# Seven block products in place of eight in a feed-forward layer on one core

## The chip, the core and the metric

The kernel runs on one core of a Trainium2 chip. TensorE (PE) multiplies; its weight loads are PEld. VectorE (DVE), ScalarE (ACT) and GpSimd (POOL) work element by element, and SyncE's queue (SPq) issues the transfers. Each engine runs its own list of instructions in order and waits on semaphores for the others. The metric is device time in microseconds (us). All matmuls of this text multiply 128 x 128 weights with a stream of 256 to 576 columns.

## The reference

One layer of a decoder with two groups of tokens, 512 of a prompt and 64 of samples (8 sequences of 8). After two mixers come the two lines that matter here, with `D_MODEL = 1024` and `D_FF = 4096`, and the last norm:

```
f = relu(rmsnorm(h, ln2_g) @ w_ff1)     # h: 576 x 1024, w_ff1: 1024 x 4096
y = h + (f * f) @ w_ff2                 # w_ff2: 4096 x 1024
y = rmsnorm(y, ln_f_g)
```

## The kernel before

Everything is float32, held as two rounded parts: hi is the value as PE's 32-bit format (F32R) rounds it, and lo the rest. `split` (L105 to L107) makes them, ACT the hi by a copy (L106), DVE the lo by a subtraction (L107). A product takes three matmuls, hi by hi, hi by lo and lo by hi; all of them are issued by `mm` (L95). A weight piece of 128 x 512 is loaded (`raw`) and split into a unit `wu` of 2 x 512 columns.

The 576 tokens stand as columns of Hh and Hl (hi and lo of the normed h, 128 x 8 x 576). The feed-forward runs in 8 chunks of 512 hidden columns, 4 blocks `m` of 128. In a chunk, **up** (the first product) makes for each block and for each half of the tokens (288 columns) one PSUM sum over 8 blocks `k`: 4 x 2 x 8 x 3 = 192 matmuls of 288 columns. `square` (L1053 to L1062) turns the sums into relu squared, split into Fh and Fl; POOL stacks hi and lo of the 64 sample tokens side by side in Fst. **down** (the second product) makes, for each half `nh` of the 1024 output columns, sums of 512 columns for four token tiles of 128 (12 matmuls each) and for the sample tile, tile 4 (8 matmuls): 112 matmuls of 512 columns. `acc` adds a sum to the residual R[t] on DVE (L968); for tile 4 it takes an ACT copy (L971, `atmp`), a DVE add (L973, `atm2`) and a POOL add (L974).

The last chunk takes the tiles one by one, tile 4 first, both halves, and after each tile `last_norm`: ACT squares R[t] into `y` with a running sum (L1036), DVE and POOL make the reciprocal root (L143, L145), DVE scales into y (L1038) and SPq stores it. `y` has two buffers; the last tile uses buffers of its own, `yh`, and works in halves.

What sets the order: the framework simulates the program when it is built and writes each engine's list from that; the waits follow from the buffers. A pool gives a tag so many buffers, and a new tile in a buffer waits for the last user of the old one, a store included. The pools of this part: 8 buffers for units of the first weight, 8 for units of the second, 7 for `raw`, 2 for each tag of `evp` (atmp, atm2).

Of the kernel before, what the change touches and what calls it, by code (L numbers as in the profile page):

```python
# [90 lines left out]
def _body(ctx, tc, nc, I, O):  # L91
# [851 lines left out]
    pools['wraw'] = tpool("wraw2", 7)  # L943
    evp = tpool("evp", 2)
# [70 lines left out]
    def last_norm(t, final):
        rows = tsz[t]
        if final:

            y = [rp.tile([128, 512], F32, name="yh", tag=f"yh{h}", bufs=1) for h in range(2)]
            q = rp.tile([128, 512], F32, name="yq", tag="yq", bufs=1)  # L1020
            s2 = rp.tile([128, 2], F32, name="ss2", tag="ss2", bufs=1)
            ss = rp.tile([128, 1], F32, name="ssf", tag="ssf")
            for h in range(2):
                x = R[t][:, h * 512:h * 512 + 512]
                act.activation(q[:rows], x, AF.Square, accum_out=s2[:rows, h:h + 1])
                (dve if h else pool).tensor_tensor(y[h][:rows], x, gf[:rows, h * 512:h * 512 + 512], op=ALU.mult)
            dve.tensor_tensor(ss[:rows], s2[:rows, 0:1], s2[:rows, 1:2], op=ALU.add)
# [138 lines left out]
```

## Time and profile before

| | us |
|---|---|
| median of 3 runs | 828.01 (827.09 to 829.6) |
| profiled execution | 827.65 |
| its span | 825.9 |
| PE busy | 789.6 (96% of the span) |
| DVE busy | 442.7 (54%) |
| ACT busy | 353.4 (43%) |
| POOL busy | 176.7 (21%) |
| mean granted clock of PE | 0.987 |

The span is one execution from its first instruction to its last; 1.75 us lie around it in the profiled execution's time. Busy time of PE counts pipelined matmuls to their modelled ends, so that a busy PE may still be slowed by its operands. The feed-forward's 8 chunks lie from about 397 us to 818 us; the last norms follow.

### The profile page before, as it was taken

Reading aid. Unit: us, or ns where it says so; the run is one execution under the profiler, and the core shown is the slowest. Engines: PE = TensorE matmul, PEld = TensorE weight load, DVE = VectorE, ACT = ScalarE, POOL = GpSimd, SP = SyncE. Lnnn points to the kernel's source line nnn. Section 1 sums busy time; section 2 is a strip of 40 time slices with the busy share of each in tenths; the row PEclk is TensorE's granted clock in tenths of the full one; section 3 lists DMA queues with packets and bytes.
Section 4 is the critical chain, followed back from the end, with each engine's and each line's share of the span. In section 5 each row is a group of like instructions: output and inputs, shape, how many; then the busy total and the mean of one; then the engine's idle time right before and its main releaser. Section 6 shows DMA issues by size and latency. Waiting matters only on the chain.

```text
span 825.9 us, 13167 instructions
## 1 busy us (share of the span) xinstructions
PE 789.6 (96%) x4825; PEld 685.8 (83%) x4825; DVE 442.7 (54%) x980; ACT 353.4 (43%) x864; POOL 176.7 (21%) x219
## 2 busy tenths in 40 slices
PE   6989999999997998999989999999999999999996
PEld 5879888878675776778888998989989899898985
DVE  5345878888962347443756345163452634435325
ACT  6535478787842243432634232232322324232213
POOL 1103744454310116010211111111111111111112
PEclk9999999999997999999999999999999999999999
DMA  9771422000967545533324132041320413303003
GB/s 317 201 207 30 135 54 52 2 2 27 327 234 264 194 118 195 194 120 115 121 85 150 54 102 75 29 153 52 102 88 16 154 52 102 102 15 100 2 1 115
DMA packets 55187, 92.05 MB, mean 111 GB/s; under 512 B 7858, under 2 KB 19090, under 8 KB 54994
## 3 DMA queue, kind: packets, MB, share of 16 engines
q1 hardware_dynamic: 54866, 91.14, 34.8%
q8 instruction: 38, 0.62, 0.3%
q14 instruction: 27, 0.22, 0.1%
q0 software_dynamic: 256, 0.07, 0.0%
HBM read 86.92 MB, written 8.39 MB: 115 GB/s over the span
## 4 chain that ended last, share of the span: by engine, by line
PE 83%; DVE 7%; DMA 3%; ACT 3%; issue 2%; POOL 1%; POOLq 0%; SPq 0%; DVEq 0%; ACTq 0%
PE acc L95 52%; PE pcs L95 6%; PE pd L95 5%; PE o L95 4%; PE pu L95 3%; PE pq L95 3%; PE s L95 2%; PE tp L692 2%; DMA raw<-in_w_in 2%; DVE wu L107 1%; PE pc L95 1%; POOL wu L107 1%; DVE Q L522 1%; POOL rstd L145 1%; DMA raw<-in_w_ff 1%
## 5 line engine op out<-in xcount | busy, mean ns | idle before, releaser
L95 PE MATMUL acc<-Hh,wu 128*128 128x288 f32 x1024 | 204.9, 295 | 0.2 <-ACT Hh L106 0.2
L106 ACT ACTIVATE wu<-raw 128x512 fp32r<-128x512 f32 (+1 forms) x184 | 105.5, 614 | 152.6 <-PE acc L95 119.5
L95 PEld LDWEIGHTS acc<-Hh,wu 128*128 128x128 f32 x1024 | 164.3, 188 | 0.7 <-ACT Hh L106 0.4
L95 PE MATMUL acc<-wu,Fh 128*128 128x512 f32 x512 | 155.5, 389 | 0.0
L95 PE MATMUL acc<-Hl,wu 128*128 128x288 f32 x512 | 150.7, 295 | 0.0
L107 DVE TENSOR_TENSOR wu<-raw,wu 128x512 fp32r<-128x512 f32 x160 | 105.2, 695 | 47.2 <-ACT wu L106 47.2
L95 PEld LDWEIGHTS acc<-wu,Fh 128*128 128x128 f32 x512 | 95.7, 188 | 19.5
L95 PE MATMUL acc<-wu,Fl 128*128 128x512 f32 x256 | 97.1, 389 | 0.0
L95 PEld LDWEIGHTS acc<-Hl,wu 128*128 128x128 f32 x512 | 96.0, 188 | 0.3
L1059 DVE TENSOR_TENSOR f<-relu 128x576 f32<-128x576 f32 x32 | 24.2, 756 | 117.9 <-ACT relu L1058 117.9
L968 DVE TENSOR_TENSOR OTp<-acc,OTp 128x512 f32<-128x512 f32 x72 | 47.7, 687 | 62.4 <-PE acc L95 62.4
L1058 ACT ACTIVATE relu<-acc 128x288 f32<-128x288 f32 x64 | 26.2, 409 | 116.9 <-PE acc L95 116.9
L974 POOL TENSOR_TENSOR R<-atm,R 64x512 f32<-64x512 f32 x18 | 30.5, 1700 | 155.1 <-DVE atm L973 155.1
L95 PE MATMUL pd<-wu,AH 128*128 128x512 f32 (+1 forms) x192 | 55.2, 371 | 8.7 <-ACT wu L106 8.2
L95 PE MATMUL pcs<-G,w 128*128 128x256 f32 x256 | 61.5, 396 | 0.0
L1061 POOL CAST Fst<-Fh 128x64 fp32r<-128x64 f32 x32 | 23.5, 734 | 175.2 <-ACT Fh L106 118.7
L95 PEld LDWEIGHTS pcs<-G,w 128*128 128x128 f32 x256 | 49.7, 199 | 10.5 <-issue 3.6
L95 PEld LDWEIGHTS acc<-wu,Fl 128*128 128x128 f32 x256 | 48.1, 188 | 10.0
L95 PEld LDWEIGHTS pd<-wu,AH 128*128 128x128 f32 x192 | 34.7, 193 | 14.8 <-ACT wu L106 8.6
L668 ACT ACTIVATE P<-s,nm 128x32 f32<-128x32 f32 (+4 forms) x88 | 40.5, 464 | 14.5 <-DVE nm L667 14.0
L95 PE MATMUL acc<-wu,Hh 128*128 128x512 f32 x128 | 40.6, 397 | 0.0
L107 POOL TENSOR_TENSOR wu<-raw,wu 128x512 fp32r<-128x512 f32 (+1 forms) x24 | 30.8, 1301 | 44.2 <-ACT wu L106 44.2
(329 smaller groups left out, 1349.5 us busy)
## 6 DMA issues: line engine op xcount, KB each, us to landing
raw<-in_w_ff SPq DMA_DIRECT2D x128, 256.0 KB
G<-in_cache_kv SPq DMA_DIRECT2D x64, 256.0 KB
raw<-in_w_in SPq DMA_DIRECT2D x32, 256.0 KB
raw<-in_w_out SPq DMA_DIRECT2D x16, 256.0 KB
out_wins<-in_state_win_kv SPq DMA_DIRECT2D x8, 504.0 KB
xt<-in_x_t SPq DMA_DIRECT2D x8, 288.0 KB
x<-in_x_prompt SPq DMA_DIRECT2D x4, 512.0 KB
KW<-in_win_kt SPq DMA_DIRECT2D x4, 512.0 KB
```

Source lines behind the costliest of these rows:

```text
L95: pe.matmul(out, lhsT, rhs, start=start, stop=stop, skip_group_check=not first_in_bank)
L106: act.activation(hi, src, AF.Copy)
L107: eng.tensor_tensor(lo, src, hi.bitcast(F32), op=ALU.subtract)
L145: pool.tensor_tensor(r[:rows], ms[:rows], mhalf[:rows], op=ALU.pow)
L522: dve.tensor_tensor(Q[b, h, c0:c1], src, Q[a, h, c0:c1].bitcast(F32), op=ALU.subtract)
L668: act.activation(p_[:, c0:c0 + w], src, AF.Exp, bias=nm[:, br, g:g + 1], accum_out=l[:, br, g:g + 1])
L692: pe.transpose(t_[:w, g * 128:(g + 1) * 128], P[g][:, c0:c0 + w], ident)
L968: dve.tensor_tensor(R[t][:, c0:c0 + 512], p, R[t][:, c0:c0 + 512], op=ALU.add)
L974: pool.tensor_tensor(R[4][:, c0:c0 + 512], tm2, R[4][:, c0:c0 + 512], op=ALU.add)
L1058: act.activation(r[:, i * 288:i * 288 + 288], p[:, :288], AF.Relu)
L1059: dve.tensor_tensor(f2, r, r, op=ALU.mult)
L1061: pool.tensor_copy(Fst[:, m, 0:64], Fh[:, m, 512:576].bitcast(F32))
```

## The change

From the second chunk on, up is done by Strassen's scheme in Winograd's form: two blocks `m` of the hidden columns, two halves of `k` and the two halves of the tokens make 2 x 2 blocks, and seven products of 4 `k` blocks take the place of eight. The token sums T1, T2, T4 and T3 (which overwrites the second half of the tokens' upper `k`) are made once, on DVE and ACT, after the up of chunk 0: for each of 4 `k`, 14 DVE operations of 288 columns and 4 ACT copies. The weight sums are made for each pair of blocks: two loads of 512 KB (`fraw`), four DVE sums of 512 columns, and seven splits. The seven results are put together on DVE in `seven`. Chunk 0 stays as it was, but with its squares by halves.

To make room, buffers shrink: 6 `raw`, one buffer for each tag of `evp`, 6 units of the second weight in a ring (a chunk still uses 8), 8 units of the first weight in a ring (a pair uses 7), one `fraw` pair, and one buffer `y` for all five last norms, the final one too. The weight sum `s3` and the final norm's scratch `yq` take the tag `atmp`. The order of two sums of the out projection before the feed-forward is changed. The last tile's second half is done in two quarters of 256 columns.

```diff
-    pools['wraw'] = tpool("wraw2", 7)
-    evp = tpool("evp", 2)
+    pools['wraw'] = tpool("wraw2", 6)
+    evp = tpool("evp", 1)
-    fw2a = tpool("fw2a", 6)
-    fw2 = [fw2a] * 6 + [fw2b] * 2
+    fw2a = tpool("fw2a", 4)
+    fw2 = [fw2a] * 4 + [fw2b] * 2
+    ring, ring2 = itertools.cycle(fw), itertools.cycle(fw2)
...
-        for t, nh in ((0, 0), (1, 0), (2, 0), (3, 0), (0, 1), (1, 1), (2, 1), (3, 1), (4, 0), (4, 1)):
+        for t, nh in ((0, 0), (1, 0), (2, 0), (3, 0), (4, 0), (0, 1), (1, 1), (2, 1), (3, 1), (4, 1)):
...
+    def token_sums(k):
...
+        t1 = sub2((0, 1), (0, 0))
+        split(T[0][0][:, k], T[0][1][:, k], t1)
+        t2 = sub1((1, 1), t1)
+        split(T[1][0][:, k], T[1][1][:, k], t2)
+        t4 = sub1((1, 0), t2)
+        split(T[2][0][:, k], T[2][1][:, k], t4)
+        t3 = sub2((1, 1), (0, 1))
+        split(Hh[:, k, N2:NT], Hl[:, k, N2:NT], t3)
+    def weight_sums(m0):
+        raw = []
+        for i in range(2):
+            r = rp.tile([128, 4, 256], F32, name="fraw", tag=f"fraw{i}", bufs=1)
+            sp.dma_start(r, w_ff1[i * 512:i * 512 + 512, m0 * 128:m0 * 128 + 256].rearrange("(k p) m -> p k m", p=128))
+            raw.append(r)
+        us = [next(ring).tile([128, 2, 512], F32R, name="wu", tag="w") for i in range(7)]
...
+        s3 = evp.tile([128, 512], F32, name="s3", tag="atmp").rearrange("p (k m) -> p k m", k=4)
+        put(0, a11)
+        dve.tensor_tensor(s3, a11, a21, op=ALU.subtract)
+        dve.tensor_tensor(a21, a21, a22, op=ALU.add)
+        dve.tensor_tensor(a11, a21, a11, op=ALU.subtract)
+        put(1, a11)
+        put(2, s3)
+        put(3, a21)
+        put(4, a12)
+        dve.tensor_tensor(a12, a12, a11, op=ALU.subtract)
+        put(5, a22)
+        put(6, a12)
...
-            y = [rp.tile([128, 512], F32, name="yh", tag=f"yh{h}", bufs=1) for h in range(2)]
-            q = rp.tile([128, 512], F32, name="yq", tag="yq", bufs=1)
+            y = rp.tile([128, D], F32, name="y", tag="y", bufs=1)
+            y = [y[:, h * 512:h * 512 + 512] for h in range(2)]
+            q = evp.tile([128, 512], F32, name="yq", tag="atmp")
...
-        y = rp.tile([128, D], F32, name="y", tag="y")
+        y = rp.tile([128, D], F32, name="y", tag="y", bufs=1)
...
+        def seven(m):
+            us = weight_sums(c * KC + m)
...
+            def prod(p, i, x, more=False):
+                for k in range(4):
+                    wh, wl = (us[i][:, s, k * 128:k * 128 + 128] for s in range(2))
+                    for j, (w, y) in enumerate(((wh, x[0]), (wh, x[1]), (wl, x[0]))):
+                        mm(p, w, y[:, k], not more and k == 0 and j == 0, k == 3 and j == 2, not more)
...
+            prod(a, 0, half(H, 0, 0))
+            p1 = fs("p1")
+            act.activation(p1, a, AF.Copy)
+            prod(b, 1, T[1])
+            u = fs("u2")
+            dve.tensor_tensor(u, b, p1, op=ALU.add)
+            prod(cc, 2, half(H, 0, 1))
+            v = fs("v")
+            dve.tensor_tensor(v, cc, u, op=ALU.add)
+            prod(d, 3, T[0])
+            dve.tensor_tensor(v, d, v, op=ALU.add)
+            out(v, 1, 1)
+            prod(a, 4, half(H, 1, 0), True)
...
+            prod(cc, 5, T[2], True)
...
+            prod(d, 6, half(H, 1, 1), True)
...
+        if c == 0:
+            for k in range(4):
+                token_sums(k)
...
             for t in (4, 0, 1, 2, 3):
-                for nh in range(2):
-                    down(t, nh, vs[nh])
+                down(t, 0, vs[0])
+                for c0, n in (((0, 256), (256, 256)) if t == 3 else ((0, 512),)):
+                    down(t, 1, vs[1], c0, n)
                 last_norm(t, t == 3)
```

The products are called P1 to P7 here, P1 being `prod(a, 0, ...)` and P7 `prod(d, 6, ...)`.

**Between two chunks, DVE.** Before, DVE's list goes from the last sums of a down through units of the coming weights (wu_6084 to wu_6099) and the sample tile's add (L973) to the first square of the next chunk:

```order
L107 TENSOR_TENSOR wu_6084<-raw_6082,wu_6084 128x512
L107 TENSOR_TENSOR wu_6089<-raw_6087,wu_6089 128x512
L107 TENSOR_TENSOR wu_6094<-raw_6092,wu_6094 128x512
L973 TENSOR_TENSOR atm2_5710<-acc_5699,atmp_5708 64x512
L107 TENSOR_TENSOR wu_6099<-raw_6097,wu_6099 128x512
L1059 TENSOR_TENSOR f2_5857<-relu_5856 128x576
L107 TENSOR_TENSOR Fl_5754<-f2_5857,Fh_5753 128x576
```

Of the change, at the start of chunk 3, wu_6652 to wu_6737 are units of the second weight; s3_6351, the two lines on fraw_6340 (L1066, L1067) and wu_6345 (the unit of P2) follow the sample tile's add:

```order
L107 TENSOR_TENSOR wu_6652<-raw_6650,wu_6652 128x512
L107 TENSOR_TENSOR wu_6657<-raw_6655,wu_6657 128x512
L107 TENSOR_TENSOR wu_6732<-raw_6730,wu_6732 128x512
L973 TENSOR_TENSOR atm2_6334<-acc_6323,atmp_6332 64x512
L107 TENSOR_TENSOR wu_6737<-raw_6735,wu_6737 128x512
L1065 TENSOR_TENSOR s3_6351<-fraw_6340 128x512
L1066 TENSOR_TENSOR fraw_6340<-fraw_6340,fraw_6342 128x4x128
L1067 TENSOR_TENSOR fraw_6340<-fraw_6340 128x4x128
L1072 TENSOR_TENSOR fraw_6342<-fraw_6342,fraw_6340 128x4x128
L107 TENSOR_TENSOR wu_6345<-fraw_6340,wu_6345 128x512
L107 TENSOR_TENSOR wu_6346<-s3_6351,wu_6346 128x512
L107 TENSOR_TENSOR wu_6347<-fraw_6340,wu_6347 128x512
```

The weight sums now stand behind the add of the sample tile, whose `atmp` holds the buffer that `s3` takes, and all units but those of P1 and P5 stand behind them.

**In the last down, PE.** Before, each token tile's two sums follow each other, and each is finished before the next begins (acc_8438 and acc_8452 are one tile, acc_8475 the next):

```order
L95 MATMUL acc_8438<-wu_8304,Fh_8048 128x512 x2
L95 MATMUL acc_8438<-wu_8304,Fl_8049 128x512
L95 MATMUL acc_8452<-wu_8309,Fh_8048 128x512 x2
L95 MATMUL acc_8452<-wu_8309,Fl_8049 128x512
L95 MATMUL acc_8452<-wu_8314,Fh_8048 128x512 x2
L95 MATMUL acc_8452<-wu_8314,Fl_8049 128x512
L95 MATMUL acc_8452<-wu_8319,Fh_8048 128x512 x2
L95 MATMUL acc_8452<-wu_8319,Fl_8049 128x512
L95 MATMUL acc_8452<-wu_8324,Fh_8048 128x512 x2
L95 MATMUL acc_8452<-wu_8324,Fl_8049 128x512
L95 MATMUL acc_8475<-wu_8289,Fh_8048 128x512 x2
```

Of the change, wu_8604 and wu_8609 are the last two units of the second half; acc_8626 is the sum of tile 4, acc_8663, acc_8700 and acc_8737 those of tiles 0 to 2, and acc_8774 the first quarter of tile 3, all of the second half:

```order
L95 MATMUL acc_8760<-wu_8589,Fh_8269 128x512 x2
L95 MATMUL acc_8760<-wu_8589,Fl_8270 128x512
L95 MATMUL acc_8626<-wu_8604,Fst_8271 128x512
L95 MATMUL acc_8663<-wu_8604,Fh_8269 128x512
L95 MATMUL acc_8700<-wu_8604,Fh_8269 128x512
L95 MATMUL acc_8737<-wu_8604,Fh_8269 128x512
L95 MATMUL acc_8774<-wu_8604,Fh_8269 128x256
L95 MATMUL acc_8626<-wu_8604,Fst_8271 128x512
L95 MATMUL acc_8626<-wu_8609,Fst_8271 128x512
L95 MATMUL acc_8663<-wu_8604,Fh_8269 128x512
L95 MATMUL acc_8663<-wu_8604,Fl_8270 128x512
L95 MATMUL acc_8663<-wu_8609,Fh_8269 128x512
```

The first halves (acc_8760 is the last of them) all stand ahead of these two units, and the second halves of all five tiles end side by side, in the last 40 matmuls of the list.

**The last norms, ACT.** Before, from the sample tile's copies to the end:

```order
L971 ACTIVATE atmp_8336<-acc_8327 64x512
L971 ACTIVATE atmp_8350<-acc_8341 64x512
L1036 ACTIVATE y_8356,ssf_8355<-R4_4295 64x1024
L1036 ACTIVATE y_8393,ssf_8392<-OTp_80 128x1024
L1036 ACTIVATE y_8430,ssf_8429<-OTp_80 128x1024
L1036 ACTIVATE y_8467,ssf_8466<-OTp_80 128x1024
L1025 ACTIVATE yq_8505,ss2_8506<-OTp_80 128x512 x2
L1029 ACTIVATE yh_8503<-yh_8503,rstd_8515 128x512
```

Of the change, with y_8641, y_8678, y_8715, y_8752 and y_8802 in one buffer one after another (OTp_80 holds R[0] to R[3]):

```order
L971 ACTIVATE atmp_8635<-acc_8626 64x512
L1091 ACTIVATE yq_8803,ss2_8804<-OTp_80 128x512
L1102 ACTIVATE y_8641,ssf_8640<-R4_4294 64x1024
L1091 ACTIVATE yq_8803,ss2_8804<-OTp_80 128x256 x2
L1102 ACTIVATE y_8678,ssf_8677<-OTp_80 128x1024
L1102 ACTIVATE y_8715,ssf_8714<-OTp_80 128x1024
L1102 ACTIVATE y_8752,ssf_8751<-OTp_80 128x1024
L1095 ACTIVATE y_8802<-y_8802,rstd_8815 128x512
```

The squares stand in the same order of tiles; each of them now writes into the buffer that the store before it reads.

## Rows read from the trace of the kernel before

**Rows 1.** The page, part 1 (busy us, share of the span, instructions) and part 4's shares by line

```profile
PE 789.6 (96%) x4825; PEld 685.8 (83%) x4825; DVE 442.7 (54%) x980; ACT 353.4 (43%) x864; POOL 176.7 (21%) x219
...
PE acc L95 52%; PE pcs L95 6%; PE pd L95 5%; PE o L95 4%; PE pu L95 3%; PE pq L95 3%; PE s L95 2%; PE tp L692 2%; DMA raw<-in_w_in 2%; DVE wu L107 1%; PE pc L95 1%; POOL wu L107 1%; DVE Q L522 1%; POOL rstd L145 1%; DMA raw<-in_w_ff 1%
```

**Rows 2.** The chain of waits, in order of time: start us, us, engine, what, line

```profile
407.30 5.02 DMA raw<-in_w_ff
...
421.01 386.70 PE acc L95 x2312
...
809.69 2.95 DMA out_ys<-y
```

**Rows 3.** A stretch from 421 to 808 us: length, busy time by engine, PEclk, DMA

```profile
421.00:808.00 387.00, 386.99 (x2315) 353.69 (x2316) 166.57 (x256) 118.64 (x227) 59.38 (x81) 1.00 0.23 72
```

**Rows 4.** Timeline of PE, first product, 564 us: start us, us, engine, line, operation

```profile
564.45 0.43 PE L95 MATMUL acc<-Hh,wu 128*128 128x288 f32 x2
...
564.84 0.42 PE L95 MATMUL acc<-Hh,wu 128*128 128x288 f32 x2
```

**Rows 5.** Timeline of PE, second product, 560 us

```profile
560.33 0.62 PE L95 MATMUL acc<-wu,Fh 128*128 128x512 f32 x2
...
561.01 0.62 PE L95 MATMUL acc<-wu,Fh 128*128 128x512 f32 x2
```

**Rows 6.** Timeline at the end of a chunk, 460 us

```profile
460.68 1.98 PE L95 MATMUL acc<-wu,Fst 128*128 128x512 f32 x8
...
462.50 0.29 PE L95 MATMUL acc<-Hh,wu 128*128 128x288 f32 x1
...
462.92 0.58 ACT L971 ACTIVATE atmp<-acc 64x512 f32<-64x512 f32 x1
...
463.81 0.68 DVE L973 TENSOR_TENSOR atm<-acc,atmp 64x512 f32<-64x512 f32 x1
```

**Rows 7.** Groups by form, 421 to 808 us: count, busy us, mean ns, idle before

```profile
L107 DVE TENSOR_TENSOR wu<-raw,wu 128x512 fp32r<-128x512 f32 x112 | 72.3, 686 | 32.1 <-ACT wu L106 32.1
...
L106 ACT ACTIVATE wu<-raw 128x512 fp32r<-128x512 f32 x112 | 64.2, 621 | 117.5 <-PE acc L95 117.4
...
L1058 ACT ACTIVATE relu<-acc 128x288 f32<-128x288 f32 x62 | 25.4, 409 | 116.9 <-PE acc L95 116.9
```

**Rows 8.** Groups by form, the whole span, DVE

```profile
L515 DVE TENSOR_TENSOR qf<-pq,rb 128x288 f32<-128x288 f32 x8 | 3.6, 455 | 0.4 <-PE pq L95 0.2
```

**Rows 9.** Timeline of DVE, four operations in a row, 437 us

```profile
437.72 2.52 DVE L107 TENSOR_TENSOR wu<-raw,wu 128x512 fp32r<-128x512 f32 x4
```

**Rows 10.** Timeline of the end, 803 us to the end

```profile
803.66 2.54 POOL L974 TENSOR_TENSOR R<-atm,R 64x512 f32<-64x512 f32 x2 [7.44 <-DVE atm L973]
...
804.59 0.39 PE L95 MATMUL acc<-wu,Fl 128*128 128x512 f32 x1
...
805.02 0.69 DVE L968 TENSOR_TENSOR OTp<-acc,OTp 128x512 f32<-128x512 f32 x1 [0.84 <-PE acc L95]
...
812.74 1.06 ACT L1036 ACTIVATE y<-OTp 128x1024 f32<-128x1024 f32 x1 [4.32 <-DMA out_ys<-y]
...
814.81 1.28 DVE L1038 SCALAR_TENSOR_TENSOR y<-OTp,rstd,gf 128x1024 f32<-128x1024 f32 x1
...
816.83 1.30 POOL L1026 TENSOR_TENSOR yh<-OTp,gf 128x512 f32<-128x512 f32 x1
...
818.19 0.39 PE L95 MATMUL acc<-wu,Fl 128*128 128x512 f32 x1
...
821.74 0.72 ACT L1029 ACTIVATE yh<-yh,rstd 128x512 f32<-128x512 f32 x1 [1.11 <-POOL rstd L145]
```

**Rows 11.** Stretches of 1 us: length, busy by engine, PEclk, DMA share, GB/s

```profile
329.00:330.00 1.00, 0.00 (x0) 0.00 (x0) 1.00 (x1) 0.56 (x1) 1.00 (x2) 1.00 0.89 290
...
331.00:332.00 1.00, 1.00 (x5) 1.00 (x6) 0.23 (x1) 0.00 (x0) 0.63 (x1) 0.50 0.41 66
...
334.00:335.00 1.00, 1.00 (x6) 0.90 (x5) 0.00 (x0) 0.00 (x0) 0.00 (x0) 0.98 0.97 307
```

More of the change, by code (lines that the diff above doesn't have):

```diff
@@ L1011, in _body, with q, tmp, sub2 @@
     KC = 4
+    N2 = NT // 2
+    tp_ = ctx.enter_context(tc.tile_pool(name="tsum", bufs=1))
+    T = [[tp_.tile([128, 4, N2], F32R, name=f"T{i}{j}") for j in "hl"] for i in (1, 2, 4)]
+    def token_sums(k):
+        def q(a, i, j):
+            return a[:, 4 * i + k, j * N2:j * N2 + N2].bitcast(F32)
+        def tmp(name):
+            return rp.tile([128, N2], F32, name=name, tag="fs", bufs=6)
+        def sub2(b, a):
+            x, y = tmp("tx"), tmp("ty")
+            dve.tensor_tensor(x, q(Hh, *b), q(Hh, *a), op=ALU.subtract)
+            dve.tensor_tensor(y, q(Hl, *b), q(Hl, *a), op=ALU.subtract)
+            dve.tensor_tensor(x, x, y, op=ALU.add)
+            return x
+        def sub1(b, x):
+            z = tmp("tz")
+            dve.tensor_tensor(z, q(Hh, *b), x, op=ALU.subtract)
+            dve.tensor_tensor(z, z, q(Hl, *b), op=ALU.add)
+            return z
+        t1 = sub2((0, 1), (0, 0))
[6 more added lines that the diff above has]
+        split(Hh[:, k, N2:NT], Hl[:, k, N2:NT], t3)
@@ new lines, in weight_sums, with put @@
+    def weight_sums(m0):
[5 more added lines that the diff above has]
+        us = [next(ring).tile([128, 2, 512], F32R, name="wu", tag="w") for i in range(7)]
+        def put(i, src):
+            v = us[i].rearrange("p s (k m) -> p s k m", k=4)
+            split(v[:, 0], v[:, 1], src)
+        (a11, a21), (a12, a22) = ([raw[i][:, :, m * 128:m * 128 + 128] for m in range(2)] for i in range(2))
+        s3 = evp.tile([128, 512], F32, name="s3", tag="atmp").rearrange("p (k m) -> p k m", k=4)
[10 more added lines that the diff above has]
+        put(6, a12)
+        return us
@@ L1017, in last_norm @@
         if final:
-            y = [rp.tile([128, 512], F32, name="yh", tag=f"yh{h}", bufs=1) for h in range(2)]
-            q = rp.tile([128, 512], F32, name="yq", tag="yq", bufs=1)
-            s2 = rp.tile([128, 2], F32, name="ss2", tag="ss2", bufs=1)
+            y = rp.tile([128, D], F32, name="y", tag="y", bufs=1)
+            y = [y[:, h * 512:h * 512 + 512] for h in range(2)]
+            q = evp.tile([128, 512], F32, name="yq", tag="atmp")
+            s2 = rp.tile([128, 3], F32, name="ss2", tag="ss2", bufs=1)
             ss = rp.tile([128, 1], F32, name="ssf", tag="ssf")
[L1023 to L1027, printed above, removed]
+            for i, (c0, n) in enumerate(((0, 512), (512, 256), (768, 256))):
+                x = R[t][:, c0:c0 + n]
+                act.activation(q[:rows, :n], x, AF.Square, accum_out=s2[:rows, i:i + 1])
+                (dve if i else pool).tensor_tensor(y[i > 0][:rows, c0 % 512:c0 % 512 + n], x, gf[:rows, c0:c0 + n], op=ALU.mult)
+            dve.tensor_reduce(ss[:rows], s2[:rows], axis=AX, op=ALU.add)
             r = rstd_of(rp, ss, D, rows)
@@ L1042, in _body @@
     for c in range(32 // KC):
-        us = [load_unit(fw[k], w_ff1[k * 128:(k + 1) * 128, c * 512:c * 512 + 512], 512) for k in range(8)]
+        if c == 0:
+            us = [load_unit(next(ring), w_ff1[k * 128:(k + 1) * 128, c * 512:c * 512 + 512], 512) for k in range(8)]
         Fh = fp.tile([128, KC, NT], F32R, name="Fh", tag="Fh")
@@ L1061, in square, with stack, half, fs @@
+                dve.tensor_tensor(r, r, r, op=ALU.mult)
+                sl = slice(i * N2, i * N2 + N2)
+                split(Fh[:, m, sl], Fl[:, m, sl], r)
+            stack(m)
+        def stack(m):
             pool.tensor_copy(Fst[:, m, 0:64], Fh[:, m, 512:576].bitcast(F32))
             pool.tensor_copy(Fst[:, m, 64:128], Fl[:, m, 512:576].bitcast(F32))
+        def seven(m):
+            us = weight_sums(c * KC + m)
+            a, b, cc, d = (bank()[:, :N2] for i in range(4))
+            def half(x, i, j):
+                return [y[:, 4 * i:4 * i + 4, j * N2:j * N2 + N2] for y in x]
+            H = (Hh, Hl)
+            def prod(p, i, x, more=False):
[3 more added lines that the diff above has]
+                        mm(p, w, y[:, k], not more and k == 0 and j == 0, k == 3 and j == 2, not more)
+            def fs(name):
+                return rp.tile([128, N2], F32, name=name, tag="fs", bufs=6)
+            def out(x, i, j, square=True):
+                if square:
+                    act.activation(x, x, AF.Relu)
+                act.activation(x, x, AF.Square)
+                sl = slice(j * N2, j * N2 + N2)
+                split(Fh[:, m + i, sl], Fl[:, m + i, sl], x)
+            prod(a, 0, half(H, 0, 0))
[11 more added lines that the diff above has]
+            prod(a, 4, half(H, 1, 0), True)
+            r = fs("c11")
+            act.activation(r, a, AF.Relu)
+            out(r, 0, 0, False)
+            prod(cc, 5, T[2], True)
+            w = fs("c21")
+            dve.tensor_tensor(w, cc, u, op=ALU.add)
+            out(w, 1, 0)
+            stack(m + 1)
+            prod(d, 6, half(H, 1, 1), True)
+            w = fs("c12")
+            dve.tensor_tensor(w, d, u, op=ALU.add)
+            out(w, 0, 1)
+            stack(m)
@@ L1070, in _body, with down @@
                 square(m0 + m, pab[m])
-        def down(t, nh, vs):
-            p = bank()
+        if c == 0:
+            for k in range(4):
+                token_sums(k)
+        def down(t, nh, vs, c0=0, n=512):
+            p = bank()[:, :n]
+            vs = [v[:, :, c0:c0 + n] for v in vs]
             for m in range(KC):
```

25 lines of the change are left out of this document (13 added, 12 removed).

## The prediction

> **What bounds the kernel now.** I read first the page's busy shares and its chain by line [rows 1]: PE is busy in 96% of the span, and half of the chain is one line, the sums of the feed-forward. Then the chain in order of time [rows 2]: from 421 us on a single piece of 386.7 us, 2312 matmuls without a wait, up to the last norms. Then that stretch by engine [rows 3]: PE busy 386.99 of 387.00 us at full granted clock, DVE 166.6, ACT 118.6. So in the feed-forward only PE counts, and each matmul taken away is time won as long as PE goes on without waits; the other two engines have slack as an average, which says nothing on the moments at which PE depends on them.
>
> The pace of PE: three matmuls of 288 columns take 0.39 us, from the starts of two groups that are three matmuls apart [rows 4], 0.1305 each over longer stretches. Three of 512 take 0.68, 0.227 each [rows 5]. By a straight line through both, one of 256 takes 0.117 (an estimate).
>
> **1. Matmuls removed.** Up was 192 matmuls of 288 for a chunk, 96 for a pair of blocks. Seven products of 4 x 3 are 84. In 14 pairs 168 go: 168 x 0.1305 = 21.9 us. The last tile's quarters: 24 x 0.117 in place of 12 x 0.227, +0.1. All of it is on the path [rows 3]. **-21.8.**
>
> **2. Chunk 1, the token sums.** They are 56 DVE operations of 128 x 288, which stand in DVE's list among the evictions of chunk 0's down. From the end of chunk 0's up to the sum (L1066) that P2, P4 and P7 of chunk 1 need, DVE has 54 operations of 288 and 20 of 512. One of 288 alone took 0.455 [rows 8], one of 512 0.686 [rows 7], in a row 0.63 [rows 9]; in a row I take 0.06 off the first too, 0.39. So 33.7 us (54 x 0.39 + 20 x 0.63) to 38.3 (0.455, 0.686), and I take 35.5, since most stand back to back. PE has for that time 112 x 0.227 + 12 x 0.1305 = 27.0 of work. The next sum and ACT's copy (0.62 [rows 7]) follow, so PE stands about 9.5 us (7.7 to 12.5). Then the second pair: its two loads of 512 KB go to the same single `fraw`, so they are issued only when the first pair's splits have read it. The nearest row is a load that held the chain for 5.02 us [rows 2]; the first pair's products cover part of it, and I take 4.5 more (0 to 6). **+14 (8 to 18).**
>
> What so long a stand does to the clock is seen once in the trace: PE had nothing from 329 to 330 us, at 331 it ran at 0.50, the lower level, 1.2 GHz, and from 334 on at 0.98 again [rows 11]. Some 3 us at half speed and the slices beside them lose 1.7. **+1.7**, once, here.
>
> **3. The start of chunks 2 to 7.** `s3` takes the buffer of the sample tile's `atmp`, of which there is one now, so DVE makes the weight sums of a chunk's first pair only after the last eviction of the chunk before. Let D be the end of the last down. Before, at this place the next matmul came with no gap, 462.50 after eight that began at 460.68 (8 x 0.227 = 1.82) [rows 6]: the units were there. Now: ACT's `atmp` D+0.2 to 0.8 and DVE's `atm2` to 1.5 (0.58 and 0.68 [rows 6]; an evicting engine starts 0.04 after PE's modelled end, 805.02 against 804.59 + 0.39 [rows 10]); one more unit 2.2; s3 2.8; L1066 3.4; L1067 4.1 (0.63 each); ACT's copy of P2's unit 4.75, those of P3 and P4 0.55 later each; DVE's parts 5.4, 6.0, 6.6. Only P1 and P5 (12 x 0.1305 = 1.57 each) have units from earlier.
> - Chunks 3, 5, 7: P5 is second in PE's list. It waits for ACT's copy of P1's sum (0.41 [rows 7]) and ends at D+3.8; P2 starts at 4.7, waits for its lo part until 5.4, and the first five products end at 9.7 in place of 7.8. With a little for the second pair 2.2 lost.
> - Chunks 2 and 6: P3 is second, on s3: it starts at D+3.45 (1.9 lost). Here the second pair's P1 stands in the list ahead of P6, and its load can be issued only at about D+7; 3.3 to 5 us later and a copy, D+12 or so, PE has waited 2.3 more. 4.2.
> - Chunk 4: P2 is second: D+4.7 in place of 1.6, and its halves; 3.4.
>
> 3 x 2.2 + 2 x 4.2 + 3.4 = 18.4. At least 7 (six times 1.2, if P5 and the second pair's load fit everywhere and nothing stands ahead of s3); at most 27 (4.5 each, a load of 5.02 us on PE's path in each). **+18.4.** Nothing hides this: the engines' slack lies later in the chunk, and the order of DVE's list is fixed.
>
> **4. The end.** A chunk uses 8 units of the second weight and has 6 buffers, so the last two units (of the last output half) come when the first half's sums have been read through. All five tiles end together. Let E be the start of the last matmul plus 0.23; before, E was 818.42 [rows 10] and the span's end, 825.9, came 7.5 later; the last ACT operation started at 821.74, 4.16 before the end.
> Now tile 4's sum is done at E-3.0 (6 x 0.227 + 14 x 0.117 before the end). Its copy, a DVE eviction ahead of it, the add and POOL's add (1.27, 2.54 for two [rows 10]) bring its norm's square to E+0.35. From the start of a square to the end of DVE's scaling is 3.35 us (812.74 to 814.81 + 1.28 [rows 10]), then the store. The row of before shows the same wait: a square that came 2.95 us after its issue, when a store of 256 KB had freed y [rows 2, 10], with two buffers. The stores of tiles 0 to 2 have 512 KB; I take 2.95 for them too. With one buffer nothing of this overlaps: tile 4's y is free at E+6.65, and each further tile takes 6.35 (3.35 + 2.95 + 0.05): 13.0, 19.35, 25.7. Then the final tile's multiplication on POOL, which now needs y as well (1.30 [rows 10]): 27.0, and the 4.16 from its scaling to the end: E+31.2. Against E+7.5: **+23.7**. It would be 22.3 if tile 4's chain is done earlier by its POOL part, 24.3 if a store of 512 KB takes 0.15 more each.
>
> **5. The rest at nothing.** The loads of fewer `raw` buffers: the same bytes, and PE's waits of 3 hold more than they cost. The order of the out projection's sums: the same sums, the rows of that stretch show no wait that it removes; 0, within 1 either way. Seven adds, squares and splits for a pair on DVE and ACT lie beside its 84 matmuls (11 us) and the down, with DVE idle in 57% and ACT in 69% of this stretch before [rows 3]; where they come late, they are counted in 3.
>
> The profiled execution took 827.65, of which 825.9 is the span; the runs' median is 828.01, so 0.36 more, which I leave. **827.65 - 21.8 + 14 + 1.7 + 18.4 + 23.7 = 863.7, so 864.** With all low ends 827.65 - 21.8 + 8 + 7 + 22.3 = 843, with all high ones 877.
>
> **The rivals.**
> *The clock falls at every chunk.* PE stands for 1 to 4 us in each of the six chunks of 3; in the row from 329 to 330 us PE did nothing, and by 331 it was at 0.50 [rows 11]. Six times 1.7 is 10.2: **874**. For: that idle stretch was no longer than the stands of 3. Against: most stands here are cut in two by a product.
> The Trainium skill, in "TensorE: Matmul & The Clock Gate", section "HAM oscillation — how this bites in real kernels", tells of a kernel whose every tile of work was followed by a wait for data, and each of whose tiles then began at the low clock, so that the price was paid once per tile. By that rule the time would be this rival's; the trace shows the fall after an idle stretch, but none repeated from chunk to chunk, since before has no waits there.
>
> *Only the end is serial.* The waits of 2 and 3 are filled by down matmuls that PE's list holds ready, as the order has some between the second pair's products: 827.65 - 21.8 + 23.7 = **829.6** (to 843 with the low ends). Against: at the start of a chunk the list holds nothing between P1 and the sums.
>
> *Shared single buffers cost nothing* (the other side): each new user of `atmp` and of `y` comes late by itself, because its own data hold it, and the sharing never decides. Then the 18.4 of 3 and the 23.7 of 4 go, and 827.65 - 21.8 + 14 + 1.7 = **822**, faster. It decides as long as the sharing costs under 6.1 us in all. For it: DVE has more than half of this stretch free [rows 3]. Against: the row at 812.74, where a square waited for a store though there were two buffers [rows 10].
>
> That the change doesn't do what it says can be left out: 84 matmuls stand where 96 stood.
>
> **How the numbers follow.** The sum with its bounds (843 to 877): 0.65. The clock falls at every chunk (870 to 887): 0.15. Only the end (829 to 843): 0.09. Shared buffers free (820 to 826): 0.05. A loss that I don't see, above 887: 0.04; a gain that I don't see, below 825: 0.02. The range leaves out the last three and most of "only the end" and takes the rest: 840 to 884. What a measurement can tell from no change is 0.3%, 2.5 us. Faster: the shared buffers and the unseen gain, 0.07; the same: the lower edge of "only the end", 0.05; slower 0.88.
>
> **What would show it.** In the profile after: 168 matmuls fewer; PE with a gap of about 9 us near 430 us and at the lower clock behind it; in each later chunk, right behind the sample tile's eight matmuls, 12 matmuls and then a gap that ends with ACT's copy of a unit; at the end four stores, each square starting when the store before has landed, some 6.35 us apart, and PE idle for 31 us. It is wrong if PE runs on between chunks (then 3 falls), or if the squares at the end lie closer than a store's time (4 falls). If PEclk is near 0.50 at each chunk's start, the first rival was right.

## The result, and the profile after

The changed kernel took 893.57 us (median of 4, 892.54 to 893.97), against 827.85 for the kernel before: 1.0782 of it, with a 95% interval from 1.0756 to 1.0808. That is 66 us slower; I had forecast 36, in a range that ended at 884. The profiled execution took 892.54, its span is 890.8.

First the page, parts 1 and 4 by engine, as in [rows 1]:

```profile
PE 791.6 (89%) x4669; PEld 682.4 (77%) x4669; DVE 544.7 (61%) x1214; ACT 419.1 (47%) x1026; POOL 184.7 (21%) x219
...
PE 71%; DVE 14%; DMA 5%; ACT 4%; issue 4%; POOL 1%; POOLq 0%; DVEq 0%; SPq 0%; ACTq 0%
```

PE has 156 matmuls fewer in the records (some are missing in either trace; the program has 156 fewer too: 168 less, 12 more by the quarters) and yet 2 us more busy time, which is what a slower clock looks like. Then the chain in order of time; the one piece of 386.7 us of [rows 2] has fallen into one or two for each chunk, with other engines in between, and at the end there are three stores on it:

```profile
426.50 30.25 PE acc L95 x192
...
493.92 37.18 PE acc L95 x202
...
537.83 8.93 PE acc L95 x46
...
547.89 38.42 PE acc L95 x212
...
593.83 45.32 PE acc L95 x250
...
863.09 2.95 DMA out_ys<-y
869.43 2.65 DMA out_yp<-y
875.54 2.64 DMA out_yp<-y
```

Two stretches by engine (length, busy us, and the granted clock as third number from the end). The first is that of [rows 3], where PE was busy in all of 387.00; the second holds chunks 2 to 7:

```profile
421.00:808.00 387.00, 355.19 (x1992) 319.33 (x1990) 244.15 (x444) 165.65 (x350) 61.01 (x69) 0.95 0.22 69
...
532.29:860.00 327.71, 303.94 (x1693) 273.18 (x1691) 200.52 (x347) 142.06 (x299) 46.58 (x61) 0.95 0.22 68
```

In chunks 2 to 7 PE is idle for 23.4 us (the stretch ends 0.3 us behind the last matmul), and the granted clock is 0.95 on the mean. It is at the lower level, 1.2 GHz, behind the gaps in each of the six chunks; 2 us of each, chunk 2 first:

```profile
536.80:538.80 2.00, 0.97 (x4) 0.98 (x5) 2.00 (x4) 1.54 (x3) 0.00 (x0) 0.50 0.11 39
594.90:596.90 2.00, 2.00 (x10) 2.00 (x10) 1.41 (x3) 1.18 (x3) 0.00 (x0) 0.50 0.03 9
646.20:648.20 2.00, 1.56 (x6) 1.54 (x7) 1.58 (x3) 2.00 (x5) 0.00 (x0) 0.50 0.00 0
700.80:702.80 2.00, 1.04 (x3) 0.74 (x4) 2.00 (x4) 2.00 (x5) 0.00 (x0) 0.50 0.03 8
758.70:760.70 2.00, 2.00 (x10) 2.00 (x10) 2.00 (x4) 0.75 (x2) 0.00 (x0) 0.50 0.05 12
813.30:815.30 2.00, 2.00 (x10) 2.00 (x9) 1.61 (x3) 1.39 (x4) 0.00 (x0) 0.50 0.00 0
```

Where the 64.9 us of the two spans lie follows from the start of the first matmul of 288 columns in each chunk (the first gap-free one of [rows 6] is at 462.50 before; after it is 471.08), the end of the last matmul and the end of the span:

| stretch | before | after | difference |
|---|---|---|---|
| start to chunk 1 | 462.50 | 471.08 | +8.6 |
| chunk 1 | 50.84 | 61.21 | +10.4 |
| chunks 2 to 7 | 305.24 | 327.38 | +22.1 |
| last matmul to the end | 7.3 | 31.1 | +23.8 |

A chunk of seven products needs 50.85 - 24 x 0.1305 = 47.7 us if PE never waits. So chunk 1 lost 13.5 us, and chunks 2 to 7, of 55.2, 52.8, 55.3, 56.3, 54.2 and 53.6 us, lost 40.8 together, over the 286.6 that their matmuls need. Of these 40.8, PE stood for 23.4; for the rest it was busy longer, 303.9 us in place of 286.6, which is 17.3 more. Some 14 of the 17.3 are the lower clock, an estimate: half of the 28 us that PE was busy in stretches at 0.50.

### The profile page after: what moved, and what is told of

Read it like the earlier page. It is cut to its first block, busy times and chain, and to the rows that moved or that the text cites. A ratio compares the mean times of both kernels' runs of the same rounds, so it can differ in the third digit from the quotient of the medians.

```text
span 890.8 us, 13110 instructions
## 1 busy us (share of the span) xinstructions
PE 791.6 (89%) x4669; PEld 682.4 (77%) x4669; DVE 544.7 (61%) x1214; ACT 419.1 (47%) x1026; POOL 184.7 (21%) x219
## 4 chain that ended last, share of the span: by engine, by line
PE 71%; DVE 14%; DMA 5%; ACT 4%; issue 4%; POOL 1%; POOLq 0%; DVEq 0%; SPq 0%; ACTq 0%
PE acc L95 43%; PE pcs L95 7%; PE pd L95 5%; PE o L95 3%; DVE wu L107 3%; PE pu L95 3%; PE pq L95 3%; PE s L95 2%; PE tp L692 2%; DMA raw<-in_w_in 2%; DVE fraw L1066 1%; DMA raw<-in_w_out 1%; ACT wu L106 1%; DMA fraw<-in_w_ff 1%; PE pc L95 1%
## 5 line engine op out<-in xcount | busy, mean ns | idle before, releaser
L95 PE MATMUL acc<-wu,Fh 128*128 128x512 f32 (+1 forms) x520 | 157.5, 387 | 0.0
L95 PE MATMUL acc<-Hh,wu 128*128 128x288 f32 x576 | 131.7, 310 | 24.7 <-ACT wu L106 17.1
L95 PEld LDWEIGHTS acc<-Hh,wu 128*128 128x128 f32 x576 | 100.7, 199 | 29.2 <-ACT wu L106 18.6
L95 PE MATMUL acc<-wu,Fl 128*128 128x512 f32 (+1 forms) x260 | 98.5, 386 | 0.0
L968 DVE TENSOR_TENSOR OTp<-acc,OTp 128x512 f32<-128x512 f32 (+1 forms) x73 | 49.0, 680 | 73.4 <-PE acc L95 73.4
L95 PE MATMUL acc<-Hl,wu 128*128 128x288 f32 x288 | 88.7, 308 | 0.0
L107 DVE TENSOR_TENSOR wu<-raw,wu 128x512 fp32r<-128x512 f32 x104 | 69.4, 696 | 30.9 <-ACT wu L106 30.8
L106 ACT ACTIVATE wu<-fraw 128x512 fp32r<-128x512 f32 x84 | 50.3, 624 | 70.1 <-DMA fraw<-in_w_ff 40.6
L107 DVE TENSOR_TENSOR wu<-fraw,wu 128x512 fp32r<-128x512 f32 x84 | 55.7, 683 | 9.2 <-ACT wu L106 8.9
L95 PEld LDWEIGHTS acc<-Hl,wu 128*128 128x128 f32 x288 | 57.7, 200 | 0.6
```

The lines of the kernel that those rows point to most:

```text
L95: pe.matmul(out, lhsT, rhs, start=start, stop=stop, skip_group_check=not first_in_bank)
L106: act.activation(hi, src, AF.Copy)
L107: eng.tensor_tensor(lo, src, hi.bitcast(F32), op=ALU.subtract)
L968: dve.tensor_tensor(r, p, r, op=ALU.add)
```

## How a chunk starts now

The timeline of all engines at the start of chunk 3, where D is 587.50 (start, us, engine, line, operation):

```profile
587.50 0.29 PE L95 MATMUL acc<-Hh,wu 128*128 128x288 f32 x1
...
587.92 0.58 ACT L971 ACTIVATE atmp<-acc 64x512 f32<-64x512 f32 x1
...
588.81 0.68 DVE L973 TENSOR_TENSOR atm<-acc,atmp 64x512 f32<-64x512 f32 x1
...
589.57 2.27 POOL L974 TENSOR_TENSOR R<-atm,R 64x512 f32<-64x512 f32 x1 [9.88 <-DVE atm L973]
...
590.01 0.68 DVE L1065 TENSOR_TENSOR s<-fraw 128x512 f32<-128x512 f32 x1
...
590.72 1.67 DVE L1066 TENSOR_TENSOR fraw<-fraw 128x512 f32<-128x512 f32 x1
...
592.42 0.69 DVE L1067 TENSOR_TENSOR fraw<-fraw 128x512 f32<-128x512 f32 x1
...
593.15 0.63 ACT L106 ACTIVATE wu<-fraw 128x512 fp32r<-128x512 f32 x1 [3.47 <-DVE fraw L1067]
...
593.83 0.40 PE L95 MATMUL acc<-T2h,wu 128*128 128x288 f32 x1 [2.25 <-ACT wu L106]
```

The chain is the forecast one, step for step, but P2 starts at D+6.3 and not at D+4.7. Two things are in the difference. The sample tile's copy and add end at 589.49, D+2.0, where I had 1.5. And L1066 takes 1.67, while the same line in the second pair took 0.69; it began 0.03 after s3 ended and was not done until POOL's add, which overlaps it, had ended at 591.84. PE's matmuls from 593.83 on are 0.24 us apart, at half speed; the fifth product ends at 600.5, D+13.0, and not at D+9.7.

## The end

ACT's squares and the last scaling, where a norm begins, and PE's last matmuls:

```profile
859.39 0.28 PE L95 MATMUL acc<-wu,Fl 128*128 128x256 f32 x1
...
859.80 1.06 ACT L1102 ACTIVATE y<-R 64x1024 f32<-64x1024 f32 x1 [0.64 <-POOL R L974]
...
866.12 1.06 ACT L1102 ACTIVATE y<-OTp 128x1024 f32<-128x1024 f32 x1 [4.23 <-DMA out_ys<-y]
...
872.16 1.06 ACT L1102 ACTIVATE y<-OTp 128x1024 f32<-128x1024 f32 x1 [4.90 <-DMA out_yp<-y]
...
878.56 1.06 ACT L1102 ACTIVATE y<-OTp 128x1024 f32<-128x1024 f32 x1 [5.24 <-DMA out_yp<-y]
...
886.58 0.72 ACT L1095 ACTIVATE y<-y,rstd 128x512 f32<-128x512 f32 x1 [6.88 <-POOL y L1092]
```

Steps of 6.32, 6.04 and 6.40 us (6.35 forecast), and 4.2 from the last scaling to the end, as in [rows 10].

## The experiments

Each kernel is the changed one with the edit shown, unless said otherwise. Times are medians; chunk lengths are taken as above.

**s3 in a buffer of its own.**

```diff
-        s3 = evp.tile([128, 512], F32, name="s3", tag="atmp").rearrange("p (k m) -> p k m", k=4)
+        s3 = rp.tile([128, D], F32, name="s3", tag="y", bufs=1)[:, 0:512].rearrange("p (k m) -> p k m", k=4)
```

> The changed kernel with the weight sum s3 in the (until the end unused) buffer y, so that it no longer shares one buffer with the sample tile's atmp. In the trace of the changed kernel chunks 2 to 7 last 52.8 to 56.3 us where their matmuls need 47.7 (54 in the last), 41 us over in all. Theory (the shared buffer puts the weight sums behind the last eviction, and the stand and the low clock follow from it): the chunks last 48 to 50 us, no stretch at the low clock from 540 us on until the end, 893.6 falls by 33 to 41 to 853 to 861. Rival (the load of the second pair into the single fraw, or the length of DVE's list, holds PE as well): chunks of 51 us or more, time above 873.

847.47 us, 1.024 (1.0208 to 1.0273) of before. Chunks 2 to 6 last 47.72 us each and chunk 7 48.08. Its chain has one piece from chunk 1 to the end, and its stretch from 529 to 811 us has no idle time and the full clock:

```profile
498.62 313.86 PE acc L95 x1819
```

```profile
529.00:811.00 282.00, 282.00 (x1664) 256.23 (x1663) 188.19 (x326) 133.86 (x287) 41.20 (x60) 1.00 0.24 75
```

With nothing but this buffer changed, all 40.8 us of chunks 2 to 7 are gone, the low clock and the waits on the second pair's load with them. The rival, that the single fraw or DVE's list holds PE in these chunks, is out. It gained 5 us more than the most I had given, since chunk 1 was 3.8 us shorter too (57.4), with no wait of PE in it over 1.9 us.

**Matmuls that are thrown away, in the gap.**

```diff
             act.activation(p1, a, AF.Copy)
+            if c > 1 and m == 0:
+                z = ps2.tile([128, 4, 128], F32, name="zz", tag="tr").rearrange("p a b -> p (a b)")
+                for i in range(12):
+                    k = i % 4
+                    mm(z[:, :N2], us[0][:, 0, k * 128:k * 128 + 128], Hh[:, k, 0:N2], i == 0, i == 12 - 1)
```

> The changed kernel with 12 matmuls of 288 columns into an unused bank behind the first product of each of chunks 2 to 7, work thrown away, which stands in the gap where PE waits for units. If the low clock that follows the gaps is a cost of its own (1.7 us or more per chunk), PE's matmuls behind the gaps are at 0.13 us each again and the time falls by 5 to 12 us, to 882 to 889, though 72 matmuls (9.4 us) are added. If the gaps alone count and the slow matmuls behind them come from late operands, it is the same or up to 5 us slower: 893 to 899.

894.08 us, 1.0815 (1.0768 to 1.0862): no gain. The build put the twelve of chunks 3, 5 and 7 into the down of the chunk before, so chunk 3 has none within it; but it ran at the full clock in this run. Three stretches of 6 us from D on, first of the changed kernel, then of this one:

```profile
587.50:593.50 6.00, 3.58 (x25) 3.11 (x23) 5.90 (x9) 2.28 (x5) 2.27 (x1) 1.00 0.50 175
593.50:599.50 6.00, 5.67 (x29) 5.45 (x30) 3.39 (x7) 2.58 (x6) 0.00 (x0) 0.72 0.42 138
599.50:605.50 6.00, 6.00 (x46) 5.96 (x45) 5.73 (x13) 5.03 (x12) 0.94 (x2) 1.00 0.11 37
```

```profile
585.80:591.80 6.00, 3.58 (x25) 3.11 (x23) 5.90 (x9) 2.28 (x5) 2.27 (x1) 1.00 0.52 175
591.80:597.80 6.00, 5.31 (x36) 4.85 (x36) 3.22 (x6) 1.85 (x4) 0.00 (x0) 1.00 0.42 136
597.80:603.80 6.00, 4.95 (x35) 4.72 (x36) 5.72 (x12) 5.38 (x12) 1.22 (x2) 1.00 0.13 42
```

At full clock PE did 36 matmuls in place of 29 in the second stretch, and then waited 1.2 us for a unit of the second pair; after 18 us it had done 96 where the slow one had done 100. The chunk lasted 53.20 us, 52.84 with the low clock. But the two are not the same list: by the trace, the second pair's P1 stands ahead of the first pair's P6 in this run, and behind it in the changed kernel, so that the wait of 1.2 us can be the order's and not the clock's. In chunks 2, 4 and 6, with matmuls in the gap and twelve more in the down, the clock still fell behind the gaps. So this run doesn't show what the low clock costs.

Other runs show it where PE's list in a chunk is that of the changed kernel. Chunk 2 in the changed kernel and in the run with early token sums (below), with the same waits, then chunk 3 in the changed kernel and in the run with the add on DVE (next), whose wait for P2 is 0.37 us shorter:

```profile
532.29:587.50 55.21, 51.06 (x282) 45.92 (x281) 34.93 (x61) 25.22 (x53) 8.51 (x10) 0.94 0.24 77
...
527.84:582.02 54.18, 50.03 (x281) 44.90 (x280) 35.04 (x61) 25.11 (x53) 8.52 (x10) 0.97 0.26 78
...
587.50:640.34 52.84, 50.09 (x282) 44.91 (x281) 32.65 (x57) 22.69 (x49) 6.99 (x10) 0.97 0.25 80
...
582.72:633.65 50.93, 48.55 (x281) 43.37 (x280) 32.64 (x59) 22.58 (x49) 3.05 (x8) 1.00 0.26 83
```

With less low clock chunk 2 is 1.0 us shorter, and chunk 3, wholly at the full clock, 1.5 beside the shorter wait. So in these chunks the low clock had a price of its own, and it came on top of the waits.

**The sample tile's add on DVE.**

```diff
-            pool.tensor_tensor(R[4][:, c0:c0 + 512], tm2, R[4][:, c0:c0 + 512], op=ALU.add)
+            dve.tensor_tensor(R[4][:, c0:c0 + 512], tm2, R[4][:, c0:c0 + 512], op=ALU.add)
```

> The changed kernel with the sample tile's last add (L974) on DVE in place of POOL. In its trace the sum L1066 took 1.65 us in each of chunks 2 to 7, where POOL's L974 ran beside it, and 0.69 where it didn't. Theory (the two engines hold each other up): L1066 takes 0.69 everywhere, and though DVE has one operation of 0.68 more ahead of the sums, the time is the same or up to 3 us shorter, 890 to 894. Rival (L1066 is long there by itself, by its in-place read or a wait): it stays at 1.65 and the time rises by 4 us or so.

L1066 takes 0.68 or 0.69 us in all 14 places; here that of chunk 3:

```profile
586.55 0.69 DVE L1066 TENSOR_TENSOR fraw<-fraw 128x512 f32<-128x512 f32 x1
```

The time is 886.26, more gain than expected; in the profile 6.3 us of it lie in chunks 2 to 7 (321.1 in place of 327.4) and 3.8 ahead of the feed-forward. The out projection there uses the same `acc`, so the edit reaches it too, but kernels that differ only behind it spread as far (below), so it is open whether these 3.8 are the edit's. Of the 6.3, 4.6 are PE's busy time (299.35 in place of 303.94), as less of it was at the low clock, and only the rest is shorter waits. So POOL's add is what held L1066 up. The Trainium skill says so on "SBUF — State Buffer", section "Who interferes with whom": a DVE operation with both inputs in SBUF and a POOL operation that reads SBUF shut each other out for a whole instruction. The trace agrees (1.65 and 0.69). It shows the other side too: POOL's add of 64x512, 1.27 alone [rows 10], took 11.01 beside the token sums of the changed kernel:

```profile
476.39 11.01 POOL L974 TENSOR_TENSOR R<-atm,R 64x512 f32<-64x512 f32 x1 [9.62 <-DVE atm L973]
```

**The end, in two halves.** First the last two units in the free ring of the first weight:

```diff
-            vs = [down_units(nh) for nh in range(2)]
+            vs = [down_units(0), [load_unit(p, w_ff2[(c * KC + m) * 128:(c * KC + m + 1) * 128, 512:1024], 512)
+                                  for m, p in enumerate([next(ring2), next(ring2), next(ring), next(ring)])]]
```

> The changed kernel with the last two units of the last chunk's second half in the ring of the first weight, which is free by then, so that the token tiles end one after another again; y stays single. Theory (the end needs both, tiles that end together and one y): tiles end 5.45 us apart, one norm with its store takes 6.2 to 6.35, so the chain is late by a few us only: the span ends about 12 us after the last matmul in place of 31, time 873 to 877. Rival (one y alone makes the end): the end stays at 27 us or more, time above 889.

881.95 us; the end shrinks from 31.1 to 20.7 us and not to 12. The norms still follow one another through the one y; the first step is 7.39, as the sample tile's store freed y only after 4.02 us here (2.95 in the changed kernel; why is open), the next two are 5.99 and 6.07:

```profile
849.80 1.07 ACT L1102 ACTIVATE y<-R 64x1024 f32<-64x1024 f32 x1 [2.79 <-POOL R L974]
...
857.19 1.06 ACT L1102 ACTIVATE y<-OTp 128x1024 f32<-128x1024 f32 x1 [6.24 <-DMA out_ys<-y]
```

```profile
853.09 4.02 DMA out_ys<-y
```

The first square begins 10.9 us ahead of the last matmul's end (860.70); tiles 5.45 us apart would have made it some 18 (4 x 5.45, less 3.4 from tile 4's sum to its square). So the tiles did not come apart as far as I had taken, and the chain through the one y still sets the end. Then the other half, buffers for y alone:

```diff
-        y = rp.tile([128, D], F32, name="y", tag="y", bufs=1)
+        y = rp.tile([128, D], F32, name="y", tag="fraw0" if t in (1, 4) else "fraw1", bufs=1)
```

> The changed kernel with the four first last norms writing into the two buffers of fraw in turn (free by then) and the final one into y; the tiles still end together. Theory: squares no longer wait for the store just before but for the one before that, and the last norm for none: the end shrinks from 31 to about 15 us after the last matmul, time 876 to 880. Rival (the stores themselves, or DVE and ACT, set the 6 us steps): above 887.

876.81 us, as expected; the end is 17.1 us, 2 more than expected.

**The token sums early.**

```diff
             for m in range(2):
                 square(m0 + m, pab[m])
+            if m0 == 0:
+                for k in range(4):
+                    token_sums(k, 0)
...
-                token_sums(k)
+                token_sums(k, 1)
```

With 0 it makes T1, T2 and T4, with 1 T3.

> The changed kernel with the token sums T1, T2 and T4 made between the two pairs of chunk 0, where DVE has room, and only T3 (16 of 56 DVE operations) behind its up. Theory (chunk 1's 13.5 us over 47.7 are DVE's list of token sums): chunk 1 lasts 50 to 54 us in place of 61.2, time 883 to 888. Rival (chunk 1 is held by the shared buffer as the later ones are): 56 us or more, time above 888.

886.28 us, in the range of the theory, but not for the reason given: chunk 1 is 5.0 us shorter (56.19, the rival's 56 or more) and chunk 0 4.6 longer (60.91); what remains is the front, which the edit doesn't touch (the feed-forward begins at 410.7 and not 414.8), and 2 us in chunks 2 to 7. The edit moved the loss, and did not remove it.

**The front alone, on the kernel before.**

```diff
-    pools['wraw'] = tpool("wraw2", 7)
+    pools['wraw'] = tpool("wraw2", 6)
...
-    us.append(out_units(1, fw2))
+    us.append(out_units(1, fw2[:4] + fw2[6:] + fw[:2]))
...
-        for t, nh in ((0, 0), (1, 0), (2, 0), (3, 0), (0, 1), (1, 1), (2, 1), (3, 1), (4, 0), (4, 1)):
+        for t, nh in ((0, 0), (1, 0), (2, 0), (3, 0), (4, 0), (0, 1), (1, 1), (2, 1), (3, 1), (4, 1)):
```

> The kernel before with three edits of the change alone, all ahead of the feed-forward: the out projection's second half with its last two units in the ring of the first weight, its sums in the new order, and 6 raw buffers in place of 7. Theory (these make the front longer; in the changed kernel the first product began 7.1 us later, and PE stood 9.1 us between 342 and 417 us where it stood 1.9 before): 831 to 836. Rival (the front's difference is the run's own variation, since kernels with the same front began it at 410.8 to 415.4 us): 826 to 829.

831.95 us, 1.0052 (1.0033 to 1.0071): these edits cost about 4 us. Of the 8.6 us in the profile half is theirs; the other half isn't settled. Kernels with the same front began the feed-forward between 410.7 and 415.4 us, the kernel before at 407.6 in its one profile (and not at about 397, as said ahead). Which of the three edits it is wasn't tried. Nor were other edits of the change that bear on the front: one buffer for each tag of `evp`, and Hst and g2, which now lie in the pool of the norm.

**All parts together, and a better place for the token sums.** All of the edits of the changed kernel above but the add and the throw-away matmuls:

> The changed kernel with s3 in y's buffer, the last two units in the free ring, the last norms in fraw's buffers, and T1, T2, T4 early. If the parts add up (46 for s3, some 22 for the end, some 8 for the token sums): 893.6 - 76 = 817, 812 to 822, faster than the kernel before. Rival (without the other waits PE meets the loads of the single fraw, or DVE's list is full): 825 or more.

825.14 us, 0.9983 (0.9956 to 1.001). That is the rival's time. Chunk 0 lasted 67.2 us, as PE waited 8.1 us for ACT's relu. The relu stood in ACT's list behind copies of the early token sums and of chunk 1's units, and the last such unit waited for its load:

```profile
452.52 0.63 ACT L106 ACTIVATE wu<-fraw 128x512 fp32r<-128x512 f32 x1 [2.43 <-DMA fraw<-in_w_ff]
...
453.39 1.29 ACT L1126 ACTIVATE relu<-acc 128x288 f32<-128x288 f32 x4
...
453.83 1.22 PE L95 MATMUL acc<-wu,Fh 128*128 128x512 f32 x2 [8.13 <-ACT relu L1126]
```

The same without the early token sums:

> The changed kernel with s3 in y's buffer, the last two units in the free ring and the last norms in fraw's buffers, but with the token sums as the change has them, behind chunk 0's up. From the run with s3 alone (847.5) the end takes away about 22 us: 825, 822 to 829. If making T1, T2 and T4 early gained nothing in the run of all parts (its chunk 0 lasted 67.2 us, with PE waiting 8.1 us for a square), the two times agree within 3 us; if it gained the 8 us that I had priced, this one takes 832 or more.

826.58 us, 0.9961 (0.994 to 0.9981); chunks 0 and 1 take 56.33 and 57.62, 114.0 together against 114.9. So early sums bring nothing in chunk 0, where their cost is what they save in chunk 1. The last one leaves chunk 1 at eight products and spreads the sums over chunks 0 and 1:

```diff
-        if c == 0:
+        if c < 2:
             for k in range(4):
-                token_sums(k)
+                token_sums(k, c)
...
-            if c:
+            if c > 1:
                 seven(m0)
```

> As tail_s3, but with chunk 1 by eight products as chunk 0, T1, T2 and T4 made behind chunk 0's up and T3 behind chunk 1's, and the seven products from chunk 2 on. Theory (all that is left of the change's losses beside the front is the token sums' turn on DVE, 10 us or so): chunk 1 takes 3.1 us more matmuls and no wait, chunks 0 and 1 together 107 us in place of 115, time 816 to 821, faster than the kernel before by about 1%. Rival (the token sums hold up the evictions of down or the squares wherever they stand): 825 or more.

819.95 us, 0.9881 (0.9851 to 0.9911): some 1.2% faster than the kernel before. Chunks 0 to 7 take 56.95, 50.85, five times 47.72 and 48.02, the end 8.9. Its chain has one piece for the feed-forward again, and by its page PE is busy for 12.6 us less than in [rows 1]:

```profile
427.17 376.46 PE acc L95 x2216
```

```profile
PE 777.0 (95%) x4693; PEld 671.8 (82%) x4693; DVE 535.3 (65%) x1198; ACT 408.2 (50%) x1010; POOL 176.3 (22%) x219
```

## Why the prediction was wrong

The direction and the waits held, and the sizes of 1 and 4; the sum failed in two terms, of which one alone (863.7 + 22.4) took it out of the range. Term by term: -2.2 in 2, +22.4 in 3, +0.1 in 4 and +8.6 in 5 lead from 863.7 to 892.6, with 892.54 in the profiled execution.

1. *Matmuls removed, -21.8.* Right: a chunk without waits lasts 47.72 where one of before lasts 50.85.
2. *Chunk 1, +14 and +1.7 for the clock.* 13.5 in all. That the size fits is in part luck: with s3 in a buffer of its own PE's long gap is gone and chunk 1 is 3.8 us shorter, so the shared buffer held this chunk too, which the term doesn't count. In the changed kernel the gap was there, though at 473 to 481 us and not near 430, and the clock fell behind it as in [rows 11]:

```profile
481.19 0.61 PE L95 MATMUL acc<-Hh,wu 128*128 128x288 f32 x1 [8.38 <-ACT wu L106]
```

3. *Chunks 2 to 7, +18.4, at most 27.* The step that failed: 40.8. Its cause was the one named, shown by the run in which s3 has its own buffer; what went wrong is that the term holds waits alone and lets PE run at its full pace behind them. The waits were near, 23.4 in place of 18.4. Some 3 of the 5 more are chunk 5, where PE stood for P5's unit, which I had taken as ready:

```profile
701.76 0.61 PE L95 MATMUL acc<-Hh,wu 128*128 128x288 f32 x1 [4.37 <-ACT wu L106]
```

   The rest of the 5 lies in chunks 3, 4 and 7, where L1066, 1.0 us longer beside POOL's add, and the sample tile's copy and add, 0.5 later, hold P2. PE's slower matmuls behind the waits are the other 17.3, most of it by the lower clock, which this term put at nothing and the first rival, which I set aside, at 10.2.
4. *The end, +23.7.* 23.8. The stores of 512 KB held y for 2.65 us, that of 256 KB for 2.95; the 2.95 that I took for all of them was 0.3 too much in three of them, made up for the most part by the POOL part of the last norm (1.51 and a start 0.4 late).
5. *The rest at nothing.* The second step that failed: the front took 8.6 us more. The order of the out projection's sums, the two units that wait for the ring, and one raw less cost some 4 of it, which I had put at 0 within 1 either way; I had looked at the bytes and at the sums, and not at whose slots the last two units wait for, as I did for the last down. That these slots are the reason is not shown, and the rest of the 8.6 is open.

Of the rivals, the one with the clock (874) was nearest in time, and its sign came: PEclk at 0.50 near the start of each chunk. I had held against it that most stands are cut in two by a product; that did not keep the clock up. Its price is part of the failed step. The prediction says that the fall is seen once in the trace of before; there is another, where PE was busy for 1.61 of 5.00 us:

```profile
250.00:255.00 5.00, 1.61 (x6) 1.36 (x6) 1.98 (x5) 1.91 (x5) 0.00 (x0) 0.50 0.36 118
```

The Trainium skill's rule ("TensorE: Matmul & The Clock Gate", section "HAM oscillation — how this bites in real kernels") is that the low clock comes back with every such wait and that its price adds to that of the waits. The trace agrees in all six chunks, and the price added where two runs with one list could be compared (1.0 and 1.5 us). Not every gap did it: in the run with the thrown-away matmuls chunk 3 had the same two gaps ahead of its second stretch and stayed at 1.00.

"Shared buffers cost nothing" was as far off as can be: sharing two buffers, atmp and y, was most of the loss.

## What to carry to other kernels

A buffer that two otherwise unrelated steps share puts one behind the other, and the price is not the wait alone: here PE's matmuls behind the waits took 17.3 us longer, beside 23.4 us of waits. Before paying such a price for room, look for a buffer that sleeps at that time: s3 in y's buffer, y in fraw's and two units in the other ring cost no byte and gave back 67 us. And a saving in matmuls is worth its count times its pace only once the side work that it needs has been placed where the engines that do it have room; here the chunk that stayed at eight products, at 3.1 us, hid some 9 us of side work (chunks 0 and 1 took 107.8 us in place of 114.0).

## What I had not expected of the hardware

- POOL's and DVE's operations on SBUF hold each other up: 0.69 became 1.65 us on DVE, and 1.27 became 11.01 on POOL, while DVE had no gap in its list.
- A store of 64 rows (256 KB) freed its buffer after 2.95 us (4.02 in one run), one of 128 rows (512 KB) after 2.65.
- Behind the same two gaps of PE at the start of a chunk the granted clock fell in the changed kernel (0.72 over the next 6 us) and stayed at 1.00 in another run. Where a chunk with one list ran both ways, the lower clock cost 1.0 and 1.5 us.
